# Rebalancing a mean/variance reduction over four engines, and cutting its last reads smaller

## The chip, the cores and the metric

The kernel runs on one core of one Trainium2 chip. The metric is the device time of one execution in microseconds (us). The core has five engines that matter here. PE is TensorE, DVE is VectorE, ACT is ScalarE, POOL is GpSimd, and SP issues the DMAs that bring the input in. Each runs its own queue of instructions in order, and semaphores tie the queues together.

Times in the text such as "160.7" without more are us from the start of the profiled span. The span is some 1.8 us shorter than the device time of the same run.

## The reference

```python
def setup_inputs():
    batch, seq, dim = 32, 512, 1024
    return {"x": np.random.randn(batch, seq, dim).astype(np.float32)}

def reference(x):
    mean_sq = np.mean(x**2, axis=-1)
    sq_mean = np.mean(x, axis=-1)**2
    return (mean_sq - sq_mean).astype(np.float32)
```

There are 32 x 512 = 16384 rows of 1024 f32 values, 67.1 MB. Each row gives one number, its variance. On the chip, 128 rows, one per partition, form a *column* of 512 KB, and there are 128 columns.

## The kernel before

Columns arrive in groups. Fifteen groups have 8 columns (4 MB each) and four small ones end the stream (4, 2, 1 and 1 columns). Three methods share the columns of a group:

- `nbn` columns: DVE's `bn_stats`/`bn_aggr` give mean and variance at once.
- The other columns get their sum of squares from an ACT `Square` pass with an accumulator.
- The plain sum of those comes from a DVE `reduce_sum` for `ncl` columns. For the rest PE folds a column: eight 128x128 transposes accumulate in PSUM, DVE copies the result to SBUF, and a matmul with ones adds it up.

`combine` later squares the means on ACT and subtracts on DVE.

```python
    for _ in range(15):
        add(8, 2, 4)        # columns, of them bn_stats, of them reduce_sum
    add(4, 1, 1)
    add(2, 1, 0)
    add(1, 0, 0)
    add(1, 1, 0)
    ...
    scratch = scpool.tile([P, D], mybir.dt.bfloat16)     # one tile for all passes
    ...
    for gi, (c0, ncols, nbn, ncl) in enumerate(plan):
        xt = xpool.tile([P, ncols, D], FP32, name="xt", tag=tag, bufs=bufs)  # 4 of 8 columns
        nc.sync.dma_start(out=xt, in_=col_range(c0, ncols))
        for k in range(nbn):
            ... bn_stats (two halves of 512), bn_aggr        # DVE
        for k in range(nbn, ncols):
            nc.scalar.activation(out=scratch, in_=xt[:, k, :], func=Square,
                                 accum_out=msq_stage[:, i : i + 1], ...)
        if ncl > 0:
            nc.vector.reduce_sum(...)                        # DVE
        for k in range(nbn + ncl, ncols):
            ... 8 transposes into psum_f                     # PE, f32
            nc.vector.tensor_copy(out=folded, in_=psum_f)    # DVE
            ... matmul with ones into psum_s                 # PE
        nc.vector.tensor_copy(out=pair_stage[...], in_=psum_s[:, :nt])
        if gi == 7:
            combine(0, 8, 8, 2)
        elif gi == 14:
            combine(64, 7, 8, 2)
            nc.scalar.dma_start(...)        # first output DMA, columns 0 to 119
    ... combine the last 8 columns, second output DMA
```

Of the kernel before, what the change touches and what calls it, by code (L numbers as in the profile page):

```python
# [3 lines left out]

# [4 lines left out]


@with_exitstack
def kernel(
    ctx: ExitStack,
    tc: tile.TileContext,
    x: bass.AP,
    out: bass.AP,
):
    nc = tc.nc
    P = nc.NUM_PARTITIONS  # L20
    FP32 = mybir.dt.float32

    xf = x.flatten_outer_dims()
    N, D = xf.shape
    assert N % P == 0
    ntiles = N // P
    DCH = D // P

    def col_range(c0, n):
        return dataclasses.replace(  # L30
            xf,
            offset=c0 * D,
            ap=[[ntiles * D, P], [D, n], [1, D]],
        )

    out_ji = dataclasses.replace(out, offset=0, ap=[[ntiles, P], [1, ntiles]])

    FMAX = nc.vector.BN_STATS_FMAX
    nsub = (D + FMAX - 1) // FMAX

    inv_sqrt_d = 1.0 / math.sqrt(D)

    plan = []
    c = 0

    def add(ncols, nbn, ncl):
        nonlocal c
        plan.append((c, ncols, nbn, ncl))
        c += ncols

    for _ in range(15):
        add(8, 2, 4)
    add(4, 1, 1)
    add(2, 1, 0)
    add(1, 0, 0)
    add(1, 1, 0)
    assert c == ntiles

    xpool = ctx.enter_context(tc.tile_pool(name="xpool", bufs=4))
    spool = ctx.enter_context(tc.tile_pool(name="spool", bufs=8))  # L60
    fpool = ctx.enter_context(tc.tile_pool(name="fpool", bufs=4))
    opool = ctx.enter_context(tc.tile_pool(name="opool", bufs=1))
    ppool = ctx.enter_context(tc.tile_pool(name="ppool", bufs=5, space=bass.MemoryType.PSUM))
    pspool = ctx.enter_context(tc.tile_pool(name="pspool", bufs=2, space=bass.MemoryType.PSUM))
    scpool = ctx.enter_context(tc.tile_pool(name="scpool", bufs=2))

    ident = opool.tile([P, P], FP32)
    masks.make_identity(nc, ident)
    ones = opool.tile([P, 1], FP32)
    nc.gpsimd.memset(ones, 1.0)  # L70

    pair_stage = opool.tile([P, 2, ntiles], FP32)
    msq_stage = opool.tile([P, ntiles], FP32)
    sqm_stage = opool.tile([P, ntiles], FP32)

    scratch = scpool.tile([P, D], mybir.dt.bfloat16)

    def combine(c0, ngrp, gsize, nbn):
        n = ngrp * gsize
        nc.scalar.activation(  # L80
            out=sqm_stage[:, c0 : c0 + n],
            in_=pair_stage[:, 0, c0 : c0 + n],
            func=mybir.ActivationFunctionType.Square,
            scale=1.0 / D,
        )
        if nbn == 0:
            nc.vector.tensor_tensor(  # L87
                out=pair_stage[:, 1, c0 : c0 + n],
                in0=msq_stage[:, c0 : c0 + n],
                in1=sqm_stage[:, c0 : c0 + n],  # L90
                op=mybir.AluOpType.subtract,
            )
        else:
            var_v = pair_stage[:, 1, c0 : c0 + n].rearrange(
                "p (g k) -> p g k", k=gsize
            )
            msq_v = msq_stage[:, c0 : c0 + n].rearrange("p (g k) -> p g k", k=gsize)
            sqm_v = sqm_stage[:, c0 : c0 + n].rearrange("p (g k) -> p g k", k=gsize)
            nc.vector.tensor_tensor(  # L99
                out=var_v[:, :, nbn:gsize],  # L100
                in0=msq_v[:, :, nbn:gsize],
                in1=sqm_v[:, :, nbn:gsize],
                op=mybir.AluOpType.subtract,
            )

    for gi, (c0, ncols, nbn, ncl) in enumerate(plan):
        tag = f"xt{ncols}"
        bufs = {8: 4, 4: 2, 2: 2, 1: 2}[ncols]
        xt = xpool.tile([P, ncols, D], FP32, name="xt", tag=tag, bufs=bufs)
        nc.sync.dma_start(out=xt, in_=col_range(c0, ncols))  # L110

        for k in range(nbn):
            i = c0 + k
            stats = spool.tile([P, nsub, 6], FP32)
            for s in range(nsub):
                nc.vector.bn_stats(  # L116
                    out=stats[:, s, :], in_=xt[:, k, s * FMAX : (s + 1) * FMAX]
                )
            nc.vector.bn_aggr(out=pair_stage[:, :, i], in_=stats)  # L119

        for k in range(nbn, ncols):
            i = c0 + k
            nc.scalar.activation(  # L123
                out=scratch,
                in_=xt[:, k, :],
                func=mybir.ActivationFunctionType.Square,
                scale=inv_sqrt_d,
                accum_out=msq_stage[:, i : i + 1],
            )

        if ncl > 0:
            nc.vector.reduce_sum(  # L132
                out=pair_stage[:, 0, c0 + nbn : c0 + nbn + ncl],
                in_=xt[:, nbn : nbn + ncl, :],
                axis=mybir.AxisListType.X,
            )

        nt = ncols - nbn - ncl
        if nt > 0:
            psum_s = pspool.tile([P, 8], FP32, name="psum_s")  # L140
            for k in range(nbn + ncl, ncols):
                psum_f = ppool.tile([P, P], FP32, name="psum_f")
                for ch in range(DCH):
                    nc.tensor.matmul(  # L144
                        out=psum_f,
                        lhsT=xt[:, k, ch * P : (ch + 1) * P],
                        rhs=ident,
                        is_transpose=True,
                        start=(ch == 0),
                        stop=(ch == DCH - 1),  # L150
                    )
                folded = fpool.tile([P, P], FP32)
                nc.vector.tensor_copy(out=folded, in_=psum_f)  # L153
                nc.tensor.matmul(  # L154
                    out=psum_s[:, k - nbn - ncl : k - nbn - ncl + 1],
                    lhsT=folded,
                    rhs=ones,
                    start=True,
                    stop=True,
                )  # L160
            nc.vector.tensor_copy(  # L161
                out=pair_stage[:, 0, c0 + nbn + ncl : c0 + ncols],
                in_=psum_s[:, :nt],
            )

        if gi == 7:
            combine(0, 8, 8, 2)
        elif gi == 14:
            combine(64, 7, 8, 2)
            nc.scalar.dma_start(  # L170
                out=out_ji[:, 0:120], in_=pair_stage[:, 1, 0:120]
            )

    combine(120, 1, 4, 1)
    combine(124, 1, 2, 1)
    combine(126, 1, 1, 0)

    nc.scalar.dma_start(
        out=out_ji[:, 120:ntiles], in_=pair_stage[:, 1, 120:ntiles]
    )  # L180


# [1 line left out]
_INS = ['x']  # L184
_OUTS = [((32, 512), 'float32')]


# [23 lines left out]
```

## Time and profile before

| | |
|---|---|
| time, median of 4 | 171.3 us (171.25 to 171.43) |
| one 8-column group lands every | 9.7 us |
| last 8-column group landed (semaphore times in the trace) | 150.8 |
| last column landed | 160.7 |
| last output DMA issued | 167.1 |
| end of the span | 169.5 |

The first lines are from the profile page of the kernel before. Each digit is the busy share of one fortieth of the span in tenths, and the last row is what the DMA engines moved, in GB/s.

```profile
DVE  0008859495976919779495968869494976949873
ACT  3008859394976909679494958859393966939970
DMA  6999999999999999999999999999999999999400
GB/s 201 418 449 418 456 410 449 418 441 425 441 425 433 425 418 433 433 433 433 433 433 425 433 433 433 433 433 422 441 425 433 433 433 433 422 406 401 189 15 1
```

The DMA row is full up to slice 37 and empty in the last two. The input stream sets the pace until about 159, and what comes after it is a tail without input. These are two of the costliest groups of instructions of the same page: line, engine, operation, output<-input, shapes and count, then busy us and mean ns of one, then the engine's idle time before them and what ended most of it.

```profile
L123 ACT ACTIVATE scratch<-xt 128x1024 bf16<-128x1024 f32 x95 | 100.4, 1057 | 51.4 <-DMA xt<-in_x_dram 48.5
L116 DVE BATCH_NORM_STATS2 stats<-xt 128x6 f32<-128x512 f32 x66 | 41.8, 673 | 33.4 <-DMA xt<-in_x_dram 33.4
```

Most of the idle time of both engines ends on the arrival of data, so they keep up with the stream.

The tail is read from the timeline of the kernel before (start us, duration us, engine, line, operation, count, and in brackets the idle time before it with what ended it).

```profile
153.31 4.40 DVE L132 TENSOR_REDUCE pair_stage<-xt 128x4 f32<-128x4096 f32 x1
157.74 0.43 DVE L153 COPY folded<-psum_f 128x128 f32<-128x128 f32 x2
...
159.23 3.23 PE L144 MATMUL psum_f<-ident,xt 128*128 128x128 f32 x14
161.43 0.43 DVE L153 COPY folded<-psum_f 128x128 f32<-128x128 f32 x2
162.97 1.65 PE L144 MATMUL psum_f<-ident,xt 128*128 128x128 f32 x8
163.14 0.16 DVE L161 COPY pair_stage<-psum_s 128x2 f32<-128x2 f32 x1 [0.67 <-PE psum_s L154]
165.00 0.38 PE L154 MATMUL psum_s<-ones,folded 128*128 128x1 f32 x2 [0.27 <-DVE folded L153]
165.50 1.28 DVE L116 BATCH_NORM_STATS2 stats<-xt 128x6 f32<-128x512 f32 x2
...
167.06 0.34 ACTq L178 DMA_DIRECT2D out_dram<-pair_stage  x1
```

DVE is still in the sum of four columns of the last big group when the first small group lands at 155.7, half of the last eight columns. DVE and PE then wait for each other in turn, as the brackets of the lines at 163.14 and 165.00 show. The statistics of a column that landed at 160.7 start at 165.50.

### The profile page before, as it was taken

To read this page: it belongs to the slowest core of one execution; us is meant where nothing else is said; L and a number is where in the kernel's file an instruction comes from. 1 tells how busy PE (TensorE), PEld (TensorE's weight loads), DVE (VectorE), ACT (ScalarE), POOL (GpSimd) and SP (SyncE) were. 2 spreads that over 40 slices of the span, in tenths; PEclk is the share of its full clock that TensorE was granted. 3 is DMA by queue.
4 is the path that set the end of the run, shared out by engine and by line. 5 is a ranking of instruction groups with operands and counts; after the bars stand their busy time and mean duration, and the time that the engine had idled before them with its cause. 6 is when DMAs were issued, how large, how long until landed. Compare 5 with 4: busy or idle time off the path is not lost.

```text
span 169.5 us, 1164 instructions
## 1 busy us (share of the span) xinstructions
PE 76.1 (45%) x340; PEld 68.9 (41%) x340; DVE 119.2 (70%) x172; ACT 111.3 (66%) x196; POOL 0.7 (0%) x7
## 2 busy tenths in 40 slices
PE   0008153462826228271633628163462826166790
PEld 0007152452726127270623627162352726065690
DVE  0008859495976919779495968869494976949873
ACT  3008859394976909679494958859393966939970
POOL 1000000000000000000000000000000000000000
PEclk9999955555555555555585675957655555558567
DMA  6999999999999999999999999999999999999400
GB/s 201 418 449 418 456 410 449 418 441 425 441 425 433 425 418 433 433 433 433 433 433 425 433 433 433 433 433 422 441 425 433 433 433 433 422 406 401 189 15 1
DMA packets 3029, 67.23 MB, mean 397 GB/s; under 512 B 592, under 2 KB 592, under 8 KB 848
## 3 DMA queue, kind: packets, MB, share of 16 engines
q1 hardware_dynamic: 2736, 67.11, 92.7%
q10 hardware_dynamic: 288, 0.07, 0.2%
q8 instruction: 2, 0.03, 0.1%
q14 instruction: 3, 0.02, 0.0%
HBM read 67.11 MB, written 0.07 MB: 396 GB/s over the span
## 4 chain that ended last, share of the span: by engine, by line
DMA 75%; ACT 12%; DVE 5%; PE 4%; issue 1%; SPq 0%; ACTq 0%
DMA xt<-in_x_dram 75%; ACT scratch L123 12%; PE psum_f L144 3%; DVE pair_stage L132 3%; DVE stats L116 2%; PE psum_s L154 1%; SPq L110 0%; DVE folded L153 0%; DVE pair_stage L119 0%; DVE pair_stage L161 0%; DVE pair_stage L87 0%; DVE pair_stage L99 0%; ACTq L123 0%
## 5 line engine op out<-in xcount | busy, mean ns | idle before, releaser
L123 ACT ACTIVATE scratch<-xt 128x1024 bf16<-128x1024 f32 x95 | 100.4, 1057 | 51.4 <-DMA xt<-in_x_dram 48.5
L144 PE MATMUL psum_f<-ident,xt 128*128 128x128 f32 x272 | 61.1, 415 | 38.6 <-DMA xt<-in_x_dram 38.6
L144 PEld LDWEIGHTS psum_f<-ident,xt 128*128 128x128 f32 x272 | 54.9, 225 | 40.0 <-DMA xt<-in_x_dram 26.5
L132 DVE TENSOR_REDUCE pair_stage<-xt 128x4 f32<-128x4096 f32 (+1 forms) x16 | 67.2, 4202 | 0.0
L116 DVE BATCH_NORM_STATS2 stats<-xt 128x6 f32<-128x512 f32 x66 | 41.8, 673 | 33.4 <-DMA xt<-in_x_dram 33.4
L154 PE MATMUL psum_s<-ones,folded 128*128 128x1 f32 x68 | 16.0, 335 | 50.7 <-DVE folded L153 50.7
L154 PEld LDWEIGHTS psum_s<-ones,folded 128*128 128x128 f32 x68 | 14.9, 302 | 56.4 <-DVE folded L153 56.4
L123 ACT ACTIVATION_READ_ACCUMULATOR scratch<-xt 128x1 f32 x95 | 17.7, 186 | 0.0
L161 DVE COPY pair_stage<-psum_s 128x2 f32<-128x2 f32 (+1 forms) x18 | 2.9, 159 | 13.7 <-PE psum_s L154 13.7
L153 DVE COPY folded<-psum_f 128x128 f32<-128x128 f32 x34 | 7.5, 261 | 0.4 <-PE psum_f L144 0.4
L119 DVE BATCH_NORM_AGGREGATE pair_stage<-stats 128x2 f32<-128x12 f32 x33 | 6.5, 198 | 0.0
L80 ACT ACTIVATE sqm_stage<-pair_stage 128x64 f32<-128x64 f32 (+4 forms) x5 | 1.1, 220 | 2.4 <-DVE pair_stage L161 2.4
L123 ACT ACT_TABLE_LOAD x1 | 1.3, 1283 | 0.7 <-PEq L195 0.7
L99 DVE TENSOR_TENSOR pair_stage<-msq_stage,sqm_stage 128x48 f32<-128x48 f32 (+3 forms) x4 | 0.7, 174 | 0.3 <-ACT sqm_stage L80 0.3
masks.py:199 POOL TENSOR_SCALAR_AFFINE_SELECT ident<-ident 128x128 f32<-128x128 f32 x1 | 0.3, 292 | 0.0
masks.py:197 POOL MEMSET ident<- 128x128 f32 x1 | 0.2, 204 | 0.3 <-POOLq L195 0.3
L87 DVE TENSOR_TENSOR pair_stage<-msq_stage,sqm_stage 128x1 f32<-128x1 f32 x1 | 0.2, 151 | 0.0
L195 POOL MEMSET const-bfloat16-1.0<- 128x1 bf16 x1 | 0.1, 101 | 0.0
L195 POOL MEMSET const-uint8-127<- 128x1 uint8 x1 | 0.1, 101 | 0.0
L195 POOL MEMSET const-float32-0.0<- 128x1 f32 x1 | 0.1, 98 | 0.2 <-issue 0.2
L195 POOL MEMSET const-float32-1.0<- 128x1 f32 x1 | 0.1, 98 | 0.0
L70 POOL MEMSET ones<- 128x1 f32 x1 | 0.1, 98 | 0.0
## 6 DMA issues: line engine op xcount, KB each, us to landing
xt<-in_x_dram SPq DMA_DIRECT2D x15, 4096.0 KB, 31.7
xt<-in_x_dram SPq DMA_DIRECT2D x1, 2048.0 KB, 36.2
xt<-in_x_dram SPq DMA_DIRECT2D x1, 1024.0 KB, 38.2
xt<-in_x_dram SPq DMA_DIRECT2D x2, 512.0 KB, 39.4
out_dram<-pair_stage ACTq DMA_DIRECT2D x1, 60.0 KB, 1.6
out_dram<-pair_stage ACTq DMA_DIRECT2D x1, 4.0 KB, 1.4
```

The lines of the kernel that those rows point to most:

```text
L80: nc.scalar.activation(out=sqm_stage[:, c0 : c0 + n], in_=pair_stage[:, 0, c0 : c0 + n], func=mybir.ActivationFunctionType.Square, scale=1 ...
L87: nc.vector.tensor_tensor(out=pair_stage[:, 1, c0 : c0 + n], in0=msq_stage[:, c0 : c0 + n], in1=sqm_stage[:, c0 : c0 + n], op=mybir.AluOpT ...
L99: nc.vector.tensor_tensor(out=var_v[:, :, nbn:gsize], in0=msq_v[:, :, nbn:gsize], in1=sqm_v[:, :, nbn:gsize], op=mybir.AluOpType.subtract,)
L116: nc.vector.bn_stats(out=stats[:, s, :], in_=xt[:, k, s * FMAX : (s + 1) * FMAX])
L119: nc.vector.bn_aggr(out=pair_stage[:, :, i], in_=stats)
L123: nc.scalar.activation(out=scratch, in_=xt[:, k, :], func=mybir.ActivationFunctionType.Square, scale=inv_sqrt_d, accum_out=msq_stage[:, i ...
L132: nc.vector.reduce_sum(out=pair_stage[:, 0, c0 + nbn : c0 + nbn + ncl], in_=xt[:, nbn : nbn + ncl, :], axis=mybir.AxisListType.X,)
L144: nc.tensor.matmul(out=psum_f, lhsT=xt[:, k, ch * P : (ch + 1) * P], rhs=ident, is_transpose=True, start=(ch == 0), stop=(ch == DCH - 1),)
L153: nc.vector.tensor_copy(out=folded, in_=psum_f)
L154: nc.tensor.matmul(out=psum_s[:, k - nbn - ncl : k - nbn - ncl + 1], lhsT=folded, rhs=ones, start=True, stop=True,)
L161: nc.vector.tensor_copy(out=pair_stage[:, 0, c0 + nbn + ncl : c0 + ncols], in_=psum_s[:, :nt],)
L195: nc = _bacc.Bacc("TRN2", target_bir_lowering=False, num_devices=1)
```

## The change

The intent: give idle POOL some work, take `reduce_sum` out, lighten ACT, and let the stream end in smaller pieces without PE work in them.

- 8-column groups: 4 columns by `bn_stats`, 2 by two ACT passes (`Square` and `Identity`, each with an accumulator), 2 by a new path. In it POOL squares the column to bf16, and PE folds both the column and its square.
- The last 8-column group arrives as two 4-column reads into the halves of one buffer. The stream ends with 4, 2, 1 and 1 columns, handled by DVE and ACT alone.
- Three scratch tiles in turn for ACT instead of one.

```diff
-    for _ in range(15):
-        add(8, 2, 4)
-    add(4, 1, 1)
-    add(2, 1, 0)
-    add(1, 0, 0)
+    for _ in range(14):
+        add(8, 4, 2)                    # columns, of them bn_stats, of them ACT
+    add(4, 2, 1)
+    add(4, 2, 1)
+    add(4, 2, 2)
+    add(2, 1, 1)
+    add(1, 1, 0)
     add(1, 1, 0)
@@ reads
+        if gi in (14, 15):
+            # two 2 MB reads into the halves of one 8-column buffer
+            if gi == 14:
+                xt_last = xpool.tile([P, 8, D], FP32, name="xt", tag="xt8", bufs=4)
+            xt = xt_last[:, 4 * (gi - 14) : 4 * (gi - 13), :]
@@ ACT
-        for k in range(nbn, ncols):
+        for k in range(nbn, nbn + ns):
+            scratch = sqpool.tile([P, D], BF16, name="scratch", tag="scratch")
             nc.scalar.activation(out=scratch, ... func=Square, accum_out=msq_stage[...])
+            nc.scalar.activation(out=scratch, ... func=Identity, scale=inv_d,
+                                 accum_out=pair_stage[:, 0, i : i + 1])
-        if ncl > 0:
-            nc.vector.reduce_sum(...)
@@ the folded columns
+                sq = sqpool.tile([P, D], BF16, name="sq", tag="sq")
+                nc.gpsimd.tensor_tensor(out=sq, in0=xt[:, k, :], in1=xt[:, k, :], op=mult)
                 ... 8 f32 transposes into psum_fx, copy, matmul with ones
+                ... 8 bf16 matmuls sq x identity into psum_fq, copy, matmul with ones
+            ... two tensor_scalar (x 1/D) from psum_s to pair_stage and msq_stage
@@ combine
-        elif gi == 14:
-            combine(64, 7, 8, 2)
+        elif gi == 15:
+            combine(64, 6, 8, 4)
+            combine(112, 2, 4, 2)
             (first output DMA)
```

More of the change, by code (lines that the diff above doesn't have):

```diff
@@ L21 @@
     FP32 = mybir.dt.float32
+    BF16 = mybir.dt.bfloat16
     xf = x.flatten_outer_dims()
@@ L41, with add @@
     inv_sqrt_d = 1.0 / math.sqrt(D)
+    inv_d = 1.0 / D
     plan = []
     c = 0
-    def add(ncols, nbn, ncl):
+    def add(ncols, nbn, ns):
         nonlocal c
-        plan.append((c, ncols, nbn, ncl))
+        plan.append((c, ncols, nbn, ns))
         c += ncols
-    for _ in range(15):
-        add(8, 2, 4)
-    add(4, 1, 1)
-    add(2, 1, 0)
-    add(1, 0, 0)
+    for _ in range(14):
[5 more added lines that the diff above has]
+    add(1, 1, 0)
     add(1, 1, 0)
@@ L60 @@
     spool = ctx.enter_context(tc.tile_pool(name="spool", bufs=8))
-    fpool = ctx.enter_context(tc.tile_pool(name="fpool", bufs=4))
+    sqpool = ctx.enter_context(tc.tile_pool(name="sqpool", bufs=3))
+    fxpool = ctx.enter_context(tc.tile_pool(name="fxpool", bufs=3))
+    fqpool = ctx.enter_context(tc.tile_pool(name="fqpool", bufs=3))
     opool = ctx.enter_context(tc.tile_pool(name="opool", bufs=1))
-    ppool = ctx.enter_context(tc.tile_pool(name="ppool", bufs=5, space=bass.MemoryType.PSUM))
-    pspool = ctx.enter_context(tc.tile_pool(name="pspool", bufs=2, space=bass.MemoryType.PSUM))
-    scpool = ctx.enter_context(tc.tile_pool(name="scpool", bufs=2))
+    pfx = ctx.enter_context(tc.tile_pool(name="pfx", bufs=3, space=bass.MemoryType.PSUM))
+    pfq = ctx.enter_context(tc.tile_pool(name="pfq", bufs=3, space=bass.MemoryType.PSUM))
+    pss = ctx.enter_context(tc.tile_pool(name="pss", bufs=2, space=bass.MemoryType.PSUM))
     ident = opool.tile([P, P], FP32)
     masks.make_identity(nc, ident)
+    identb = opool.tile([P, P], BF16)
+    masks.make_identity(nc, identb)
     ones = opool.tile([P, 1], FP32)
     nc.gpsimd.memset(ones, 1.0)
+    onesb = opool.tile([P, 1], BF16)
+    nc.gpsimd.memset(onesb, 1.0)
     pair_stage = opool.tile([P, 2, ntiles], FP32)
@@ L74 @@
     sqm_stage = opool.tile([P, ntiles], FP32)
-    scratch = scpool.tile([P, D], mybir.dt.bfloat16)
     def combine(c0, ngrp, gsize, nbn):
@@ L83, in combine @@
             func=mybir.ActivationFunctionType.Square,
-            scale=1.0 / D,
         )
-        if nbn == 0:
-            nc.vector.tensor_tensor(
-                out=pair_stage[:, 1, c0 : c0 + n],
-                in0=msq_stage[:, c0 : c0 + n],
-                in1=sqm_stage[:, c0 : c0 + n],
-                op=mybir.AluOpType.subtract,
-            )
-        else:
-            var_v = pair_stage[:, 1, c0 : c0 + n].rearrange(
-                "p (g k) -> p g k", k=gsize
-            )
-            msq_v = msq_stage[:, c0 : c0 + n].rearrange("p (g k) -> p g k", k=gsize)
-            sqm_v = sqm_stage[:, c0 : c0 + n].rearrange("p (g k) -> p g k", k=gsize)
-            nc.vector.tensor_tensor(
-                out=var_v[:, :, nbn:gsize],
-                in0=msq_v[:, :, nbn:gsize],
-                in1=sqm_v[:, :, nbn:gsize],
-                op=mybir.AluOpType.subtract,
-            )
-    for gi, (c0, ncols, nbn, ncl) in enumerate(plan):
+        var_v = pair_stage[:, 1, c0 : c0 + n].rearrange("p (g k) -> p g k", k=gsize)
+        msq_v = msq_stage[:, c0 : c0 + n].rearrange("p (g k) -> p g k", k=gsize)
+        sqm_v = sqm_stage[:, c0 : c0 + n].rearrange("p (g k) -> p g k", k=gsize)
+        nc.vector.tensor_tensor(
+            out=var_v[:, :, nbn:gsize],
+            in0=msq_v[:, :, nbn:gsize],
+            in1=sqm_v[:, :, nbn:gsize],
+            op=mybir.AluOpType.subtract,
+        )
+    for gi, (c0, ncols, nbn, ns) in enumerate(plan):
         tag = f"xt{ncols}"
         bufs = {8: 4, 4: 2, 2: 2, 1: 2}[ncols]
-        xt = xpool.tile([P, ncols, D], FP32, name="xt", tag=tag, bufs=bufs)
+        if gi in (14, 15):
+            if gi == 14:
+                xt_last = xpool.tile([P, 8, D], FP32, name="xt", tag="xt8", bufs=4)
+            xt = xt_last[:, 4 * (gi - 14) : 4 * (gi - 13), :]
+        else:
+            xt = xpool.tile([P, ncols, D], FP32, name="xt", tag=tag, bufs=bufs)
         nc.sync.dma_start(out=xt, in_=col_range(c0, ncols))
@@ L129 @@
             )
-        if ncl > 0:
-            nc.vector.reduce_sum(
-                out=pair_stage[:, 0, c0 + nbn : c0 + nbn + ncl],
-                in_=xt[:, nbn : nbn + ncl, :],
-                axis=mybir.AxisListType.X,
-            )
-        nt = ncols - nbn - ncl
-        if nt > 0:
-            psum_s = pspool.tile([P, 8], FP32, name="psum_s")
-            for k in range(nbn + ncl, ncols):
-                psum_f = ppool.tile([P, P], FP32, name="psum_f")
+            nc.scalar.activation(
+                out=scratch,
+                in_=xt[:, k, :],
+                func=mybir.ActivationFunctionType.Identity,
+                scale=inv_d,
+                accum_out=pair_stage[:, 0, i : i + 1],
+            )
+        ngt = ncols - nbn - ns
+        if ngt > 0:
+            psum_s = pss.tile([P, 2, 4], FP32, name="psum_s")
+            for k in range(nbn + ns, ncols):
+                slot = k - nbn - ns
+                sq = sqpool.tile([P, D], BF16, name="sq", tag="sq")
+                nc.gpsimd.tensor_tensor(
+                    out=sq, in0=xt[:, k, :], in1=xt[:, k, :], op=mybir.AluOpType.mult
+                )
+                psum_fx = pfx.tile([P, P], FP32, name="psum_fx")
                 for ch in range(DCH):
                     nc.tensor.matmul(
-                        out=psum_f,
+                        out=psum_fx,
                         lhsT=xt[:, k, ch * P : (ch + 1) * P],
@@ L151 @@
                     )
-                folded = fpool.tile([P, P], FP32)
-                nc.vector.tensor_copy(out=folded, in_=psum_f)
+                folded_x = fxpool.tile([P, P], FP32)
+                nc.vector.tensor_copy(out=folded_x, in_=psum_fx)
                 nc.tensor.matmul(
-                    out=psum_s[:, k - nbn - ncl : k - nbn - ncl + 1],
-                    lhsT=folded,
+                    out=psum_s[:, 0, slot : slot + 1],
+                    lhsT=folded_x,
                     rhs=ones,
@@ L160 @@
                 )
-            nc.vector.tensor_copy(
-                out=pair_stage[:, 0, c0 + nbn + ncl : c0 + ncols],
-                in_=psum_s[:, :nt],
+                psum_fq = pfq.tile([P, P], FP32, name="psum_fq")
+                for ch in range(DCH):
+                    nc.tensor.matmul(
+                        out=psum_fq,
+                        lhsT=sq[:, ch * P : (ch + 1) * P],
+                        rhs=identb,
+                        start=(ch == 0),
+                        stop=(ch == DCH - 1),
+                    )
+                folded_q = fqpool.tile([P, P], BF16)
+                nc.vector.tensor_copy(out=folded_q, in_=psum_fq)
+                nc.tensor.matmul(
+                    out=psum_s[:, 1, slot : slot + 1],
+                    lhsT=folded_q,
+                    rhs=onesb,
+                    start=True,
+                    stop=True,
+                )
+            nc.vector.tensor_scalar(
+                out=pair_stage[:, 0, c0 + nbn + ns : c0 + ncols],
+                in0=psum_s[:, 0, :ngt],
+                scalar1=inv_d,
+                scalar2=None,
+                op0=mybir.AluOpType.mult,
+            )
+            nc.vector.tensor_scalar(
+                out=msq_stage[:, c0 + nbn + ns : c0 + ncols],
+                in0=psum_s[:, 1, :ngt],
+                scalar1=inv_d,
+                scalar2=None,
+                op0=mybir.AluOpType.mult,
             )
         if gi == 7:
-            combine(0, 8, 8, 2)
-        elif gi == 14:
-            combine(64, 7, 8, 2)
+            combine(0, 8, 8, 4)
+        elif gi == 15:
+            combine(64, 6, 8, 4)
+            combine(112, 2, 4, 2)
             nc.scalar.dma_start(
@@ L172 @@
             )
-    combine(120, 1, 4, 1)
+    combine(120, 1, 4, 2)
     combine(124, 1, 2, 1)
-    combine(126, 1, 1, 0)
     nc.scalar.dma_start(
```

## The prediction

> **What bounds the kernel now.** The input stream. The page's slices show the DMA engines 90% or more busy from 4 us on, at about 433 GB/s; the windows view gives 423 to 439 GB/s from 13 to 153 us. A 4 MB group lands every 9.7 us (13.3, 23.1 ... 150.8 us; landings in the trace). Per 10 us DVE is busy about 7.7 and ACT 7.1 (windows), so both wait for data in every group (waits: ACT 48.5 us, DVE 33.4). Removing work in the middle gains nothing.
>
> **What can be won.** Only the tail. The last column lands at about 160.7 us, the span ends at 169.5. In between (timeline, chain of waits) DVE is late from the last 8-column group (a 4.40 us sum of four columns ends at 157.7) and then alternates with PE (14 transposes, 3.1 us, small sums, 8 more transposes). The last statistics start at 165.5, though their data landed at 160.7. The output DMA is issued at 167.06; 2.4 us follow and stay.
>
> **What the change does, per 8-column group.**
> - DVE: drops the 4.40 us sum; statistics for 4 columns instead of 2 (1.37 us each with the aggregate), four PSUM copies of 0.26, two small ones: about 6.9 us.
> - ACT: 2 columns x 2 passes at 1.18 us pitch: 4.7 instead of 7.1.
> - PE: the same 16 f32 transposes (3.65 us), plus 16 bf16 matmuls and two more sums. No trace has the bf16 ones; at half the f32 pitch (228 ns), an estimate, 1.8 us. In all about 6.8.
> - POOL: two new squares of 128x1024. The Trainium skill, "GPSIMD Engine Reference", section "Performance versus the Vector engine", gives 4497 ns for a 2048-element f32 add: an estimate of 2.25 us each; no run here shows it yet.
> All are below 9.7 us, so the middle stays DMA-bound and the last landing at 160.7, give or take 0.5. The page also says POOL shares SBUF interfaces with DVE's two-port or two-input work; statistics have one input, so I expect them not to slow.
>
> **The new tail.** The last four groups land at 155.7, 158.2, 159.5 and 160.7; no TensorE work is left after the group landing at 150.8.
> - DVE: 155.7 + 2.7, then 1.37 per column: 162.6.
> - ACT: 155.7 + 4 x 1.18 = 160.5; last two passes to 162.8; small squares and the first output DMA's issue about 0.8; DVE's subtract 0.15. ACT is the end: last output DMA at about 163.8 instead of 167.06.
> Gain 3.2 us.
>
> **Prediction: 168.1 us**, 80% range 166.5 to 170.6. Faster by over 2% (below 167.9) 0.42, within 2% 0.49, slower 0.09.
>
> **What would show each step right or wrong.** DMA slices and landings unchanged; last output DMA near 163.8, ACT passes in the chain's end, no TensorE piece there; POOL squares near 2.25 us, statistics still 673 ns, f32 transposes still 415 ns.
>
> **What would make it wrong.** (a) POOL squares over 4.8 us would bind the middle. (b) Engines run in program order: if DVE and PE wait for each other alternately after the statistics (about 6.2 + 6.8 us, estimated from the same durations), a group takes 13 us and the kernel is tens of us slower. In the trace of before both columns' transposes run ahead of the first small sum, so I expect it not to. (c) The second half-buffer read waiting for users of the first half. (d) The middle combine holding ACT or DVE in the last 10 us: then the gain shrinks to 1 or 2 us.

## The result

| | before | after |
|---|---|---|
| median, all runs | 170.93 us (169.50 to 171.48, 16 runs) | 166.96 us (166.88 to 167.09, 11 runs) |
| last column landed | 160.7 | 160.8 |
| last output DMA issued | 167.06 | 162.85 |
| end of the span | 169.5 | 165.2 |

The ratio is 0.978 (95% interval 0.975 to 0.980). Ratios are computed as the mean time of one kernel's fast runs over that of the other's of the same rounds, so not quite the ratio of the medians quoted. The interval holds 0.98, so by the 2% mark the verdict "faster" was left unclear, though the gain itself is not in doubt. The kernel before scatters over 2 us from run to run, the kernel after over 0.2 us here, and over 0.6 us together with its later control (up to 167.44, below). No run here shows the cause of that scatter.

The same rows of the page of the kernel after, with POOL's, which was empty before but for the first slice:

```profile
DVE  0007749194592938649194774909559292899694
ACT  3007246090541808245190724609154280875493
POOL 2007144080541707145080713508053170764000
DMA  6999999999999999999999999999999999999950
GB/s 206 428 444 436 413 452 413 452 436 411 444 413 452 428 421 444 415 440 428 421 452 413 444 428 421 448 415 428 436 420 452 421 428 393 432 434 424 400 198 1
```

The stream is what it was: full slices at the same rates, and the slices are shorter only because the span is. The costs per instruction, from the groups of the same page:

```profile
L119 DVE BATCH_NORM_STATS2 stats<-xt 128x6 f32<-128x512 f32 x130 | 81.0, 665 | 56.4 <-DMA xt<-in_x_dram 56.4
L148 POOL TENSOR_TENSOR sq<-xt 128x1024 bf16<-128x1024 f32 x30 | 56.2, 1893 | 94.9 <-DMA xt<-in_x_dram 94.9
L127 ACT ACTIVATE scratch<-xt 128x1024 bf16<-128x1024 f32 x33 | 34.6, 1049 | 84.5 <-DMA xt<-in_x_dram 84.5
```

A POOL square takes 1.89 us, and DVE's statistics are no slower beside it (665 against 673 ns). And this is the tail in the timeline of the kernel after:

```profile
155.70 1.88 DVE L119 BATCH_NORM_STATS2 stats<-xt 128x6 f32<-128x512 f32 x3 [0.52 <-DMA xt<-in_x_dram]
155.70 1.06 ACT L127 ACTIVATE scratch<-xt 128x1024 bf16<-128x1024 f32 x1 [0.72 <-DMA xt<-in_x_dram]
156.67 0.19 ACT L127 ACTIVATION_READ_ACCUMULATOR scratch<-xt 128x1 f32 x1
156.76 1.04 ACT L127 ACTIVATE scratch<-xt 128x1024 bf16<-128x1024 f32 x1
157.80 1.04 ACT L134 ACTIVATE scratch<-xt 128x1024 bf16<-128x1024 f32 x1
...
162.22 0.20 ACT L88 ACTIVATE sqm_stage<-pair_stage 128x2 f32<-128x2 f32 x1
162.60 0.21 DVE L122 BATCH_NORM_AGGREGATE pair_stage<-stats 128x2 f32<-128x12 f32 x1
162.85 0.34 ACTq L215 DMA_DIRECT2D out_dram<-pair_stage  x1
```

Both engines stand idle, with nothing left over, when the 4-column group lands at 155.7. DVE then works five columns without a gap and is the last to finish (162.8); ACT is done at 162.4.

### The profile page after: what moved, and what is told of

The parts are those of the page before. It is cut to its first block, busy times and chain, and to the rows that moved or that the text cites. A ratio compares the mean times of both kernels' runs of the same rounds, so it can differ in the third digit from the quotient of the medians.

```text
span 165.2 us, 1736 instructions
## 1 busy us (share of the span) xinstructions
PE 86.4 (52%) x570; PEld 76.2 (46%) x570; DVE 100.1 (61%) x292; ACT 72.9 (44%) x138; POOL 57.4 (35%) x40
## 4 chain that ended last, share of the span: by engine, by line
DMA 83%; DVE 10%; ACT 3%; SPq 1%; issue 0%
DMA xt<-in_x_dram 83%; DVE stats L119 9%; ACT scratch L127 2%; ACT scratch L134 1%; SPq L113 1%; DVE pair_stage L122 1%; DVE pair_stage L96 0%; ACT sqm_stage L88 0%
## 5 line engine op out<-in xcount | busy, mean ns | idle before, releaser
L119 DVE BATCH_NORM_STATS2 stats<-xt 128x6 f32<-128x512 f32 x130 | 81.0, 665 | 56.4 <-DMA xt<-in_x_dram 56.4
L148 POOL TENSOR_TENSOR sq<-xt 128x1024 bf16<-128x1024 f32 x30 | 56.2, 1893 | 94.9 <-DMA xt<-in_x_dram 94.9
L153 PE MATMUL psum_fx<-ident,xt 128*128 128x128 f32 x240 | 52.9, 394 | 60.5 <-DMA xt<-in_x_dram 60.5
L153 PEld LDWEIGHTS psum_fx<-ident,xt 128*128 128x128 f32 x240 | 43.9, 212 | 61.7 <-DMA xt<-in_x_dram 48.3
L127 ACT ACTIVATE scratch<-xt 128x1024 bf16<-128x1024 f32 x33 | 34.6, 1049 | 84.5 <-DMA xt<-in_x_dram 84.5
L134 ACT ACTIVATE scratch<-xt 128x1024 bf16<-128x1024 f32 x33 | 34.4, 1041 | 0.0
L172 PE MATMUL psum_fq<-identb,sq 128*128 128x128 bf16 x240 | 27.2, 283 | 2.5 <-POOL sq L148 1.4
L172 PEld LDWEIGHTS <-sq 128*128 128x128 bf16 x240 | 21.8, 130 | 8.9 <-POOL sq L148 8.2
L163 PE MATMUL psum_s<-ones,folded_x 128*128 128x1 f32 x60 | 12.1, 281 | 5.1 <-DVE folded_x L162 4.8
L163 PEld LDWEIGHTS psum_s<-ones,folded_x 128*128 128x128 f32 x60 | 10.6, 227 | 7.4 <-DVE folded_x L162 6.5
L162 DVE COPY folded_x<-psum_fx 128x128 f32<-128x128 f32 x30 | 8.3, 276 | 0.0
```

The source lines that it names most:

```text
L119: nc.vector.bn_stats(out=stats[:, s, :], in_=xt[:, k, s * FMAX : (s + 1) * FMAX])
L127: nc.scalar.activation(out=scratch, in_=xt[:, k, :], func=mybir.ActivationFunctionType.Square, scale=inv_sqrt_d, accum_out=msq_stage[:, i ...
L134: nc.scalar.activation(out=scratch, in_=xt[:, k, :], func=mybir.ActivationFunctionType.Identity, scale=inv_d, accum_out=pair_stage[:, 0, i ...
L148: nc.gpsimd.tensor_tensor(out=sq, in0=xt[:, k, :], in1=xt[:, k, :], op=mybir.AluOpType.mult)
L153: nc.tensor.matmul(out=psum_fx, lhsT=xt[:, k, ch * P : (ch + 1) * P], rhs=ident, is_transpose=True, start=(ch == 0), stop=(ch == DCH - 1),)
L162: nc.vector.tensor_copy(out=folded_x, in_=psum_fx)
```

## The experiments

Theory T: the stream ends at the same moment in both kernels, and all of the gain is made behind the last big group. Rival M: the lighter middle pays. The first runs put back one stretch of the plan at a time; their `combine` calls follow the plan and are left out of the cuts below. Line numbers in the profile lines are those of the kernel run.

### Old body for all 15 big groups, new last four groups

```diff
+        if gi < 15:      # the body of the kernel before: 2 bn_stats, 6 Square, reduce_sum of 4, 2 folds
+            ...
+            continue
-    14 x add(8, 4, 2); add(4, 2, 1); add(4, 2, 1)
+    15 x 8 columns
```

> The body of the kernel before for fifteen 8-column groups, and only the last four groups (8 columns) by the new method. Theory T (all of the gain lies behind the last big group): last landing stays near 160.7 us, the old body's sum of four keeps VectorE on the last 8-column group until about 158, five statistics columns follow, so the last output DMA is issued near 165.6 and the time is about 169.8 us. Rival M (the lighter middle is what pays): the middle is the old one, so time as before, 170.9 to 171.3.

Measured: 169.25 us (168.75 to 169.59, 6 runs), ratio to before 0.990. The last column landed at 160.8, the last output DMA was issued at 165.38. Taking PE and `reduce_sum` out of the last 8 columns alone moves the last output DMA from 167.06 to 165.38. (The run profiled was the slowest of the six.) DVE enters these columns late, at 158.19 where the first four had landed at 155.8, as the timeline of this run shows:

```profile
153.40 4.40 DVE L127 TENSOR_REDUCE pair_stage<-xt 128x4 f32<-128x4096 f32 x1
...
158.19 0.68 DVE L169 BATCH_NORM_STATS2 stats<-xt 128x6 f32<-128x512 f32 x1
```

### New body everywhere, last big group not split

```diff
-    14 x add(8, 4, 2); add(4, 2, 1); add(4, 2, 1)
+    15 x add(8, 4, 2)
```

> The kernel after, but with the last columns before 120 read as one 8-column group by the new method instead of two 4-column halves. Theory T: VectorE is done with that group about 6.45 us after it lands at 150.8, at 157.3, then five statistics columns at 1.37 us follow: last output DMA near 164.5, time about 168.6 us. Rival M: the middle is the new one, so 167.0 as the kernel after.

Measured: 168.46 us (168.36 to 168.51, 5 runs), ratio 0.986; last output DMA at 164.27. As T had it, DVE ended its work on the 8-column group at 157.2 and worked on without a pause. Against the kernel after (162.85), the split is worth 1.4 us.

### Old body for the first 14 big groups, whole new tail

```diff
+        if gi < 14:      # the body of the kernel before
+            ...
+            continue
```

> The body of the kernel before for the first fourteen 8-column groups, everything from column 112 on as in the kernel after. Theory T: as the kernel after, 167.0 us (166.7 to 167.3), last output DMA near 162.9. Rival M: most of the gain is lost, 169 us or more. Rival P (POOL's squares slow or speed the stream in the middle): differs from 167.0 by over 0.5 us.

Measured: 168.56 us (168.22 to 168.86, 6 runs), ratio 0.986. T in this form missed by 1.6 us. The time is also what rival P named, a change of over 0.5 us because POOL no longer squares in the middle. But the stream was not late (the last column landed at 160.5 against 160.8), and the next run, with POOL out of thirteen groups, speaks against P. Two lines of this run, DVE and ACT at the group that landed at 155.6 (both began at 155.70 in the kernel after), and the last output DMA:

```profile
156.74 1.87 DVE L172 BATCH_NORM_STATS2 stats<-xt 128x6 f32<-128x512 f32 x3
157.27 1.06 ACT L180 ACTIVATE scratch<-xt 128x1024 bf16<-128x1024 f32 x1 [0.65 <-DVE pair_stage L98]
164.41 0.34 ACTq L266 DMA_DIRECT2D out_dram<-pair_stage  x1
```

DVE left the last old group 2.0 us later than DVE in the kernel after left its own (149.45 against 147.4), and through two 4-column groups it did not catch up. ACT had no backlog of its own, but its queue held the small square of `combine` and the first output DMA in front of its next passes. Those waited for DVE, so ACT started 1.57 us late. That is the whole loss: the last output DMA is 1.56 us late. This trace also holds an odd line, a subtract of 128x36:

```profile
150.74 1.89 POOL L201 TENSOR_TENSOR sq<-xt 128x1024 bf16<-128x1024 f32 x1 [2.98 <-DMA xt<-in_x_dram]
151.77 0.91 DVE L98 TENSOR_TENSOR pair_stage<-msq_stage,sqm_stage 128x36 f32<-128x36 f32 x1
```

A 128x48 subtract took 0.21 us in the kernel before. This one ends as POOL's square does, and costs DVE about 0.7 us while it is trying to catch up. In the kernel after the subtract of these columns (128x24 there) came at 150.29, before POOL's square began, and took 0.17 us. So up to 0.7 of the 1.56 us may be this hold, which the lateness brought about; no run separates the two.

### Old body for the first 13 only

If it is only the lateness at the last big group that counts, thirteen old groups should be free.

```diff
-        if gi < 14:
+        if gi < 13:
```

> As e2_old_middle, but with the body of the kernel before only for the first thirteen groups; the fourteenth, the last big one, has the new body. In e2_old_middle the data landed as early as in the kernel after (160.7 against 160.8), but VectorE was 2.0 us late on the old body of the last big group (149.5 instead of 147.5) and never caught up. Theory C (what counts in the middle is only how late the last big group leaves VectorE and ScalarE): 167.0 to 167.3 us, as the kernel after. Rival M (every old group in the middle costs something): 168.4 or more, as e2_old_middle's 168.56.

Measured: 167.01 us (166.53 to 167.76, 5 runs), ratio 0.978. This is the time of the kernel after. DVE and ACT both start on the last 4-column group at 155.74, and the last output DMA goes out at 162.88. Of the rebalanced middle, thirteen groups are worth nothing that this run's scatter would show, and the fourteenth is worth 1.5 us, the held subtract included.

### One scratch tile

```diff
+    scratch = opool.tile([P, D], BF16)
-            scratch = sqpool.tile([P, D], BF16, name="scratch", tag="scratch")   # three in turn
```

> The kernel after with a single scratch tile for all ScalarE passes, as the kernel before had, instead of three in turn. My prediction took 1.18 us from one pass to the next; the kernel after shows 1.04. Theory S (passes that write the same scratch tile follow each other only every 1.18 us): spacing 1.18 again, ScalarE ends near 163.2, last output DMA near 163.4 to 163.5 instead of 162.85, time about 167.5 us. Rival F (the spacing comes from the alternation of Square and Identity, not from the tile): spacing stays 1.04, 167.0 us.

Measured: 167.57 us (167.45 to 167.75, 5 runs), ratio 0.981; last output DMA at 163.39. ACT in this run's timeline:

```profile
155.68 1.06 ACT L127 ACTIVATE scratch<-xt 128x1024 bf16<-128x1024 f32 x1 [0.71 <-DMA xt<-in_x_dram]
156.65 0.19 ACT L127 ACTIVATION_READ_ACCUMULATOR scratch<-xt 128x1 f32 x1
156.87 1.06 ACT L134 ACTIVATE scratch<-xt 128x1024 bf16<-128x1024 f32 x1
158.04 1.06 ACT L127 ACTIVATE scratch<-xt 128x1024 bf16<-128x1024 f32 x1
```

The starts are 1.18 us apart, as in the kernel before, against 1.04 with other tiles. The order of the passes changed too, to `Square` and `Identity` in turn. But the kernel before has only `Square` and shows 1.18, and the version below alternates on different tiles and shows 1.06. So it is the shared tile that costs 0.14 us per pass. The traces also show how. Behind each pass stands an `ACTIVATION_READ_ACCUMULATOR` of 0.19 us, whose record raises a semaphore. On one tile the next pass waits for that semaphore and starts at 156.87, just after the read has ended (156.83). In the kernel after, on another tile, the pass at 156.76 starts while the read that began at 156.67 still runs. The 0.14 us is the wait that orders two writes to one tile.

### POOL beside small DVE instructions

```diff
             nc.vector.bn_aggr(out=pair_stage[:, :, i], in_=stats)
+            if k == 0 and 4 <= gi < 12:
+                # groups 4 to 7: xt[:, 0, 0:8] - xt[:, 0, 8:16]; groups 8 to 11: xt[:, 0, 0:8] * (1/D)
+                nc.vector.tensor_tensor(...) if gi < 8 else nc.vector.tensor_scalar(...)
```

> The kernel after plus one tiny VectorE instruction per group, put behind the first column's statistics, while POOL squares: in groups 4 to 7 a subtract of 128x8 with two inputs in SBUF, in groups 8 to 11 a multiplication by a constant of 128x8 with one input. In e2_old_middle a 128x36 subtract took 0.91 us and ended as POOL's square ended, where 128x48 took 0.21 in the kernel before. Theory H (a VectorE instruction with two SBUF inputs is held while POOL works): the subtracts take about 0.7 us, until POOL's first square ends, or up to 2.5 us if they wait for the second too. Rival (the 0.91 us was something else): 0.15 us each. No forecast for the one-input form beyond 0.15 us if nothing holds it. The time stays within 0.3 us of 167.0, as VectorE has 3 us to spare per group.

Measured (one look): 167.09 us. The instructions of the added tile, in the view of that tile (durations in ns: smallest, median, largest), and one case of each engine from the timeline:

```profile
L126 DVE TENSOR_TENSOR tiny<-xt x4: 848/848/850, 54.9 to 84.0; 128x8 f32<-128x8 f32 x4
L133 DVE TENSOR_SCALAR tiny<-xt x4: 852/852/853, 93.7 to 122.9; 128x8 f32<-128x8 f32 x4
```

```profile
53.79 3.74 POOL L165 TENSOR_TENSOR sq<-xt 128x1024 bf16<-128x1024 f32 x2 [5.96 <-DMA xt<-in_x_dram]
54.86 0.85 DVE L126 TENSOR_TENSOR tiny<-xt 128x8 f32<-128x8 f32 x1
```

All eight are held, each until 0.03 us after the end of POOL's first square (53.79 + 1.89 = 55.68, and the subtract ends at 55.71). Theory H holds, and the one-input form is held just the same. The Trainium skill says in "GPSIMD Engine Reference", section "Specifications", that GpSimd shares its SBUF interfaces with VectorE and contends with instructions of two SBUF inputs or in a two-port mode. "Advanced Engine Details and Errata", section "VectorE Performance Modes", lists `tensor_scalar` among those that can run in a two-port mode. This agrees for the subtract; that the one-input form ran in such a mode no run shows. The statistics have one input and stay at 663 ns.

### POOL twice and three times as busy

```diff
+                for _ in range(1 if gi < 12 else 0):    # 2 in the second kernel
+                    sqd = sqpool.tile([P, D], BF16, name="sqd", tag="sqd", bufs=2)
+                    nc.gpsimd.tensor_tensor(out=sqd, in0=xt[:, k, :], in1=xt[:, k, :], op=mult)
```

> The kernel after with one idle extra square per POOL column in the first twelve groups: POOL works 4 x 1.87 = 7.5 us per group, below the 9.7 us between landings. Theory D (the middle is hidden behind the stream while every engine stays below 9.7): 167.0 to 167.3 us. Rival (POOL's traffic slows VectorE's statistics or the stream): over 167.5, statistics longer than 665 ns or landings later.

Measured: 167.12 us (167.04 to 167.19, 4 runs), ratio 0.978; last landing at 161.0. Doubling POOL's work in twelve groups costs nothing in the end. But the middle subtract of `combine`, 0.19 us long in the kernel after, was held here too, to the end of a square, while the next square followed at once:

```profile
92.72 1.89 POOL L149 TENSOR_TENSOR sqd<-xt 128x1024 bf16<-128x1024 f32 x1 [2.27 <-DMA xt<-in_x_dram]
92.94 1.72 DVE L96 TENSOR_TENSOR pair_stage<-msq_stage,sqm_stage 128x32 f32<-128x32 f32 x1 [0.32 <-ACT sqm_stage L88]
94.57 1.89 POOL L153 TENSOR_TENSOR sq<-xt 128x1024 bf16<-128x1024 f32 x1
```

> The same with two extra squares: 6 x 1.87 = 11.2 us per group, above 9.7, in twelve groups. Theory D: POOL falls behind by 1.5 us a group, 18 us in the end; the four buffers absorb nearly all of it for the stream, so the landings stay (last at 160.8), but POOL is done with the twelfth group only at about 148 us, VectorE works through the rest without a gap, and the last output DMA is issued near 172 instead of 162.9: about 176 us (173 to 179). Rival (buffers do not absorb it): landings slip too, 183 us or more.

Measured (one look): 188.32 us. Neither theory said why. The stream was on time up to the group that landed at 121.5, and the next one landed at 146.6. The rows of its page, and one line of its timeline:

```profile
POOL 2019999999999999999999999994199999830000
DMA  6999999999999999999999999400299999999400
```

```profile
104.80 23.33 DVE L96 TENSOR_TENSOR pair_stage<-msq_stage,sqm_stage 128x32 f32<-128x32 f32 x1 [0.32 <-ACT sqm_stage L88]
```

The subtract of `combine` in the middle of the kernel met a POOL that now squared without a gap, and was held for 23.3 us. It came free at 128.1, when POOL itself had to stop: its output tiles were full, because PE waited for DVE's copies. Unlike the tiny instructions above, and unlike this same subtract with POOL twice as busy, it did not slip in between two squares: twelve squares that started after it went first. In all nine cases that did slip in, POOL had been idle just before the square that held the instruction; here it had not. Whether that decides it is open.

To test this reading, the subtract was moved out of POOL's way:

```diff
-        if gi == 7:
-            combine(0, 8, 8, 4)
-        elif gi == 15:
-            combine(64, 6, 8, 4)
+        if gi == 15:
+            combine(0, 14, 8, 4)
```

> As e7_pool_thrice, but the subtract of columns 0 to 63, which that trace shows held for 23.3 us at 104.8 us while POOL squared without a gap, is joined with the one of columns 64 to 111 behind the last big group, where POOL has gaps. Theory H (the hold of the two-input subtract is what broke the stream in e7_pool_thrice): no VectorE instruction over 2 us, landings as in the kernel after (last at 160.8 to 161), POOL done with the twelfth group near 147 us, then VectorE works off two big groups at 6.5 us, two halves at 3.4 and five columns: last output DMA near 174.7, about 178 us (175 to 181). Rival (six squares per group break the stream by themselves): 186 us or more, landings late again.

Measured (one look, on another chip than the other experiments): 181.44 us, 0.4 us outside the range. The longest subtract took 0.20 us, and the last column landed at 160.6. The hold is shown as the cause of the broken stream, and four buffers do hide from it a POOL that is 15% too slow for twelve groups. The rest, 14 us, is the backlog that DVE works off at the end. Its last output DMA comes at about 177.3, 2.6 us later than I had it; that part I had sized too small and did not trace further.

### A version that beats both

The kernel after ends on DVE's backlog, which starts because four columns land at once at 155.7. So: finer reads.

```diff
-    add(4, 2, 2)
-    add(2, 1, 1)
-    add(1, 1, 0)
-    add(1, 1, 0)
+    add(2, 1, 1)
+    add(2, 1, 1)
+    add(1, 1, 0)
+    add(1, 1, 0)
+    add(1, 0, 1)
+    add(1, 1, 0)          # read as two halves of 512 elements
@@ ACT
-            nc.scalar.activation(out=scratch, ... func=Identity, ...)
+            scratch2 = sqpool.tile([P, D], BF16, name="scratch2", tag="scratch2")
+            nc.scalar.activation(out=scratch2, ... func=Identity, ...)
```

> A version meant to beat the kernel after: the last eight columns arrive as reads of 2, 2, 1, 1, 1 and 1 columns instead of 4, 2, 1, 1, the very last one as two halves of 512 elements, the last but one goes to ScalarE, and the two passes of one column write different scratch tiles. If VectorE's backlog (it worked without a gap from 155.7 to 162.8) is what ends the kernel after, it has none left when the last half lands at 160.8; VectorE ends near 161.7 and ScalarE near 161.9, last output DMA near 162.1 instead of 162.85, time 166.2 us (165.9 to 166.6). If the small reads slow the stream instead, 167 us or more.

> The kernel after once more, as the control beside v1_finer_tail on the same chip: 166.96 us within 0.2.

Measured: 166.38 us (166.27 to 166.50, 5 runs), ratio to before 0.974, beside 167.18 us (167.08 to 167.44, 4 runs) for the kernel after on the same chip. The control came 0.22 us above the forecast's 166.96, just outside its 0.2. The last half landed at 161.1, not at 160.8: the last data came 0.3 us later than in the kernel after (one trace each), and the version wins in spite of it. The tail in this version's timeline:

```profile
159.72 1.06 ACT L140 ACTIVATE scratch<-xt 128x1024 bf16<-128x1024 f32 x1 [0.91 <-DMA xt<-in_x_dram]
160.49 1.35 DVE L132 BATCH_NORM_STATS2 stats<-xt 128x6 f32<-128x512 f32 x2
160.78 1.04 ACT L148 ACTIVATE scratch<-xt 128x1024 bf16<-128x1024 f32 x1
162.37 0.34 ACTq L229 DMA_DIRECT2D out_dram<-pair_stage  x1
```

DVE's last column now begins when its first half is there. What ends this kernel is ACT's pair of passes over the column before it, with DVE close behind: ACT's last small square ends at 162.15, DVE's statistics at 162.08.

## Why the prediction was right

The time (166.96, forecast 168.1, range 166.5 to 170.6) was right, and the gain that it named, in the tail, was the one that came: the last output DMA went out 4.2 us earlier, against 3.2 forecast. Point by point:

- **The stream is the bound, and stays.** Right. The last column landed at 160.8 instead of 160.7.
- **"Removing work in the middle gains nothing."** Right for thirteen of the fourteen groups (167.01 with the old body in them), wrong for the fourteenth: its old body costs 1.5 us, because DVE carries its lateness into the tail (and meets the held subtract on the way). The boundary of "tail" lies one big group earlier than I drew it.
- **Where the gain lies.** Step by step by the last output DMA: 167.06; 165.38 with the last four groups by the new method; 164.27 with all big groups new; 162.85 with the last big one split. The times of these four kernels go the same way: 170.74 (the kernel before in those rounds), 169.25, 168.46, 166.96. So T as worded was too narrow: 1.7 of the 4.2 us is made behind the last big group, and 2.5 us by the new body (1.1) and the split (1.4) of that group itself (by the times 1.5, 0.8 and 1.5). My sum for the tail started DVE and ACT free at 155.7 without showing that they would be; they were, with only 0.52 and 0.72 us to spare.
- **ACT ends the kernel at about 163.8.** This is the step that failed. DVE ended it, at 162.8 as forecast (162.6), and ACT was done at 162.4. The term that was mis-sized first is ACT's spacing: I took 1.18 us from the trace of before, where every pass writes the same tile. With three tiles in turn it is 1.04. Putting the single tile back restores 1.18 and moves the last output DMA to 163.39. The subtract that follows ACT's work was due at about 163.7 (162.8 + 0.8 + 0.15) and done at 162.6, 1.1 us earlier. The six passes make 0.7 us of that: they ended at 162.1 instead of 162.8. The other 0.4 us is the second term: I had put the issue of the first output DMA into this tail, and it went out at 155.21, before the data. I read the line of the diff that brings in the three tiles and gave it no cost.
- **Costs.** POOL's square: 2.25 us estimated from the Trainium skill's "GPSIMD Engine Reference", 1.89 measured. The statistics, unchanged: right. Eight bf16 matmuls took 0.61 to 1.06 us in the timeline, so 16 take 1.2 to 2.1; my 1.8 lies in that range.
- **(a) POOL over 4.8 us per square binds the middle.** Two squares in place of one cost nothing. Three (5.6 us per column) cost 14 to 21 us, for a reason that I had not named: the held subtract, and DVE's backlog at the end.
- **(b) DVE and PE alternating** and **(c) the half-buffer read** did not happen. **(d) The combine holding ACT** did not happen in the kernel after, where ACT's first output DMA went out at 155.21, before the data of 155.7. It did in the run with the old middle.

## What to carry to other kernels

When a stream is the bound, time the last few landings and ask of each engine how late it enters them: work before that counts only through the lateness it leaves, here through one group out of fourteen. End such a stream in small pieces and keep work that bounces between engines out of them. When you put POOL to work beside DVE, look at each DVE instruction that falls into POOL's time. Here the statistics were not slowed, while small subtracts and a small multiplication were held to the end of a square, and once, with POOL working without a pause, for 23.3 us. Move such instructions to where POOL is idle.

## What the Trainium skill lacked or had wrong

- "GPSIMD Engine Reference", section "Performance versus the Vector engine", gives about 2.6 cycles per element as the floor with two inputs. At the page's 1.2 GHz that is 2.22 us (an estimate) for 1024 elements. POOL's square, both of whose inputs are the same f32 tile and whose output is bf16, took 1.89 us, and back to back the squares came every 1.85 us. No run here tried two different inputs or an f32 output.
- No page has this: a held DVE instruction can be passed over by POOL instructions that start after it. A 128x32 subtract waited 23.3 us while twelve later squares went first; in another run the same subtract came free at the end of one square, after 1.72 us.
- "ScalarE: Activation LUTs" has no word on the instruction that reads the accumulator after a pass (0.19 us). Passes of 128x1024 followed each other every 1.04 us where the next one did not wait for that read, and every 1.18 us where it did, for the sake of a shared output tile.
- No page gives a size for this: from the fourth to the sixth group on, in all traces kept, the last of the 16 DMA engines signalled a landing some 1.1 to 2.1 us after the middle one (160.69 against 158.99 in the kernel before), where the first three groups showed 0.4 to 0.7. The traces do not tell which engine it was.
